# Gating unit of a two-layer decoder: layer norm on ScalarE, one block sum on VectorE, and another order of the same products

## The chip, the cores and the metric

The kernel runs on one core of one Trainium2 chip. The metric is the device time of one execution in microseconds (us). Three executions of the kernel before gave 807.21, 809.53 and 811.4 us; the median is 809.53 us. A profile was taken of one further execution. The engines have short names in the profile: PE is TensorE, DVE is VectorE, ACT is ScalarE, POOL is GpSimd, SP is SyncE, which here only issues transfers.

## What is computed

Two decoder layers over 512 tokens of width 1024, batch 1, float32. Each layer norms the tokens, scales and shifts them by columns that come from a conditioning vector (`ada_w`), mixes them, and then runs a squared-ReLU MLP of width 4096. Layer 0 mixes by windowed means. Layer 1 mixes by a gating unit, and this is the part that the change is about:

```python
def sgu_mixer(h, w_in, ln_g, ln_b, w_s, b_s, w_out):
    z = gelu(h @ w_in)                      # 512 x 2048
    u, v = split(z, 2)                      # 512 x 1024 each
    v = layernorm(v, ln_g, ln_b)            # over the 1024 features of a token
    v = v.reshape(B, 4, 128, 8, 128)        # 4 chunks of 128 tokens, 8 heads of 128 features
    mixed = einsum('hts,bnshc->bnthc', tril(w_s), v) + b_s
    gated = u * mixed
    return gated @ w_out
```

## The kernel before, in words

**Precision.** A float32 product is made of three fast ones. A weight tile is split into a high part `wh` (ACT copies it to the fast type) and a low part `wl` (DVE subtracts: `wl = raw - wh`); `split` does this for one 128x1024 tile. `split_d` does it without DVE: ACT writes `wh`, ACT writes `wl = -wh` into the low part's place, and POOL issues a transfer that adds the raw weights to it (an accumulating transfer). The list `LO` names the tiles that go the second way: the units u5 and u7 of the u half, and tiles o2 and o3 of the eight tiles of the output weights.

**The v half.** `v` is made by seven block products instead of eight (a Strassen-like scheme): the units v1, v2, v5, v6, v3, v7, v4, 24 matmuls of 128x512 each. Each takes a sum of blocks of the input (`hs`, made by `h_sum` from `hq`) and a sum of blocks of `w_v`. The weight sums build up in place in the tile `VB[0, 0]`: W00 for v1, then W01 is added for v5, then W11 for v6, then W10 for v4. Before the change each addition is an accumulating transfer of 1 MB from DRAM, which POOL issues once the two splits of the last sum have been read. v3 uses W11 alone (`VB[1, 1]`), v7 uses W01 + W11 in a third tile (`VB[0, 1]`). All these tiles are called `vb` in the profile.

**The u half and what follows.** u0 to u7 are products of 24 matmuls of 128x512 (u0 and u1 in two halves `a` and `b`). After a v block has its parts, ACT takes the Gelu in place; when a token tile of 128 tokens has both halves, `v_norm` norms it. Before the change DVE does this: `bn_stats` on both halves, `bn_aggr`, a small scalar step, POOL takes the power -0.5, and DVE applies mean and scale to 128x1024. `do_mix` (steps m0 to m7) multiplies the normed tokens by the triangular matrices, 4 matmuls each into one PSUM bank; `do_gate` (g0 to g7) multiplies with u and splits the result into the pair `gt`. Then come the products with `w_o`, in two halves of 4 weight tiles (`blocks(w_o[dh], dh)`: o0 to o3, o4 to o7), each over 4 token tiles of 24 matmuls.

**Columns.** While this runs, 24 columns of `ada_w` for the MLP are reduced: SP loads a 512 KB tile called `ada`, and one DVE instruction of 128x1024 makes the dot products. Most tiles lie in the pool `w4` with three buffers, which the raw `w_o` tiles (`raw`) use too.

**What sets the order.** PE runs strictly in the order of the code, that is of the string `SEQ`. Every other engine's order is made by `Plan.run`, a list scheduler that runs when the kernel is built: it takes the recorded instructions and its own costs and due times, and hands each engine the ready instruction with the earliest due time, and so settles the in-order queues of DVE, ACT, POOL and SP. One of its rules holds DVE free around a small POOL `tensor_tensor` (the power).

Of the kernel before, what the change touches and what calls it, by code (L numbers as in the profile page):

```python
# [7 lines left out]
F32 = mybir.dt.float32  # L8
F32R = mybir.dt.float32r
AF = mybir.ActivationFunctionType  # L10
# [4 lines left out]
P = 128  # L15
D = 1024
S = 512
# [57 lines left out]
class Plan:  # L75
# [129 lines left out]
    def run(self, lead):  # L205
# [63 lines left out]
            return True  # L269

        lock = {i for i, o in enumerate(ops) if o[0] == "POOL" and o[1] == "tensor_tensor"}
        gap = {i for i in lock if any(ops[j][0] == "DVE" for j in succs[i])}
        spot = {i: k for k, i in enumerate(pe)}
        sums = [0.0]
        for i in pe:
# [54 lines left out]
        while count < N:  # L330
            moved = True
            while moved:
                moved = False
                for e in ready:
                    if e == "DVE" and any(i in gap and when[i] <= now + 1e-9 and k - cost[i][1] < now + lead["gap"] for k, i in ready["POOL"]):
                        continue
                    if free[e] > now + 1e-9 or e == "SP" and sum(x[0] for x in lines[e]) > self.QUEUED or len(lines[e]) > 6:
                        continue
                    if e == "PE":
                        pick = pe[ppos] if ppos < len(pe) and not left[pe[ppos]] and when[pe[ppos]] <= now + 1e-9 and fits(pe[ppos]) else None  # L340
                    else:
                        pick, back = None, []
                        while ready[e]:
                            k, i = heapq.heappop(ready[e])
                            if when[i] <= now + 1e-9 and fits(i) and not (e in ("DVE", "ACT") and yields(e, i)) and not (i in lock and free["DVE"] > now + 1e-9):
                                pick = i
                                break
                            back.append((k, i))
                        for x in back:
                            heapq.heappush(ready[e], x)  # L350
                    if pick is None:
                        continue
                    i = pick
                    if e == "PE":
                        ppos += 1
                    for x in self.tiles[i]:
                        if x in place and x not in opened:
                            t, _ = place[x]
                            opened.add(x)
                            nxt[t] += 1  # L360
                            held[t] += 1
                    start[i] = now
                    if ops[i][1] == "dma_start":
                        issue = 0.85 if e == "POOL" else 0.35
                        free[e] = now + issue
                        flow(now)
                        row = min(x.free_size() for x in (*ops[i][3], *ops[i][4]))
                        lines[e].append([cost[i][0] + 0.01, cost[i][0] * min(1, 2048 / row), i])
                        landing()
                        end = now + cost[i][1] + sum(x[0] for x in lines[e][:-1])  # L370
                    else:
                        free[e] = now + cost[i][0]
                        end = now + cost[i][1]
                        if i in gap:
                            free["DVE"] = now + cost[i][0]
                        heapq.heappush(events, (end, i))
                    heapq.heappush(events, (free[e], -1))
                    soon[e].discard(i)
                    for j in succs[i]:
                        if i in self.preds[j]:  # L380
                            unstarted[j] -= i not in spot
# [12 lines left out]
            if i < 0:  # L394
                continue
            done[i] = now
            count += 1
            for x in self.tiles[i]:
                togo[x] -= 1
                if not togo[x] and tag[x] in held and (x in opened or x in before[tag[x]]):  # L400
                    held[tag[x]] -= 1
            for j in succs[i]:
                if i in self.preds[j]:
                    left[j] -= 1
                    hop = now + (0.0 if ops[i][0] == ops[j][0] else self.HOP)
# [13 lines left out]
def decoder_kernel(ctx: ExitStack, tc: tile.TileContext, xtok, vecs, fgrow, ada0, ada1, pool_w, w1s, w1, w1f, w1b, w2, w_v, w_u, w_o, wsT, ws, bs, out):  # L419
# [105 lines left out]
            V.tensor_tensor(l[:, c], r[:, c], f32(h[:, c]), ALU.subtract)  # L525
        return h, l

    LO = "u5 u7 o2 o3".split()

    def split_d(r, src=None):  # L530

# [1056 lines left out]
    def v_prep(m):  # L1588

        if m == 1:  # L1590
            VB[0, 0, 0] = vb0[0]
            VB[0, 0] = two(vb0[0])
        elif m == 2:
            v_load(1, 0)
        if m in (5, 6, 3, 7):
            h_sum(m)
        b = VB[{2: (1, 0), 3: (1, 1), 7: (0, 1)}.get(m, (0, 0))]
        src = {2: (1, 0), 3: (1, 1), 1: (0, 0)}.get(m)
        w = [split_d(b[q], src and wv_at(*src, q)) if f"v{m}{q}" in LO else split(b[q]) for q in range(2)]
        if m in (1, 5, 6):  # L1600
            G.dma_start(whole_(VB[0, 0, 0]), wv_at(*CHAIN_[{1: 5, 5: 6, 6: 4}[m]]), accum_op=ALU.add)
        if m == 5:
            v_load(1, 1)
        elif m == 3:
            v_load(0, 1)
            G.dma_start(whole_(VB[0, 1, 0]), wv_at(1, 1), accum_op=ALU.add)
        return w
# [3 lines left out]
    def v_run(m, w):  # L1611
# [14 lines left out]
        for hf in range(2):  # L1626
            po = banks[hf]
            r, n = {1: (0, 0), 5: (1, 1), 6: (0, 1), 3: (0, 1), 7: (1, 1), 2: (0, 0), 4: (1, 0)}[m]
            o = vt[2 * r + hf][:, n]
            if m in (1, 5) or m in (6, 3) and "v" not in half_:  # L1630
                A.activation(o, po, AF.Copy, scale=-1.0 if m == 6 else 1.0)
                if m in (6, 3) and hf:
                    half_.append("v")
                continue
            if m in (2, 3):
                V.tensor_tensor(o, o, po, ALU.add)
            elif m in (7, 6):
                V.tensor_tensor(o, o, po, ALU.subtract)
            A.activation(o, po if m == 4 else o, AF.Gelu)

    def v_norm(t):
        v = vt[t]
        stt = sm.tile([P, 2, V.BN_STATS_DIM], F32, name="stt", tag="stt")
        for ch in range(2):
            V.bn_stats(stt[:, ch, :], v[:, ch])
        ag = sm.tile([P, V.BN_AGGR_DIM], F32, name="ag", tag="ag")
        V.bn_aggr(ag, stt)
        r = rsqrt(ag[:, 1:2], 1.0, LN_EPS, 1)
        V.tensor_scalar(v, v, ag[:, 0:1], r, ALU.subtract, ALU.mult)

    ur = hx.tile([P, 2, D], F32, name="ur", tag="hx")
    wu, pu = {}, {}
# [74 lines left out]
    h_sums()  # L1727
    ready = {}
    cols = [modulation(q, get4 if q % 2 else get_gb) for q in range(24, 32)]
    cols += [modulation(q, get4) for q in range(32, 48)]  # L1730
    SEQ = "v1 v2 u0a u1a r0 u0b v5 u1b c2 u2 v6 c2 v3 c2 r1 v7 c2 u3 c1 n0 n1 v4 c1 n2 n3 c1 u4 c1 u5 m0 u6 m1 m2 c1 m3 g0 g1 u7 m4 g2 s0 g3 m5 m6 m7 g4 g5 g6 g7".split()
    prods = [x for x in SEQ if x[0] in "vu" and not x.endswith("b")]
    rs = []
    for x in SEQ:
# [32 lines left out]
    ex = cols  # L1767
    h_[0] = hparts()
    h32.append(featurewise("h32"))
    for dh in range(2):  # L1770
        wo = blocks(w_o[dh], dh)

        early = tuple(range(KD))
        n_ = 6 if dh == 0 else KD
# [1 line left out]
        for t, ks in [(t, early[:n_]) for t in range(3)] + [(t, early[n_:]) for t in range(3)] + [(3, early)]:  # L1776
# [4 lines left out]
            if early[-1] in ks:  # L1781
                gated(t, S * dh, S, pos[t])
                for _ in range(2):
                    if ex:
                        ex.pop(0)()
                if dh == 1 and t == 2:
                    normed(0, 1, 1)
                    spill(0)
# [137 lines left out]
```

## Time and profile before

| | |
|---|---|
| median of three executions | 809.53 us (807.21 to 811.4) |
| the profiled execution | 810.57 us, of which the span of the profile is 808.8 us |
| PE busy | 785.4 us (97% of the span) |
| DVE, ACT, POOL busy | 695.1, 520.6, 106.0 us |
| mean granted PE clock | 0.995 |
| gating unit, first v product to the last product with `w_o` | 361.34 to 500.24 us of the span |

A row of the timeline gives the start and length of an instruction in us, its engine, the source line (128 is the replay of all recorded instructions), what it writes and reads, and in brackets how long the engine stood idle before it and what ended that. PE ends are modelled: a 128x512 matmul is shown with 0.38 us although the next starts 0.22 us after it.

### The profile page before, as it was taken

Reading aid. Unit: us, or ns where it says so; the run is one execution under the profiler, and the core shown is the slowest. Engines: PE = TensorE matmul, PEld = TensorE weight load, DVE = VectorE, ACT = ScalarE, POOL = GpSimd, SP = SyncE. Lnnn points to the kernel's source line nnn. Section 1 sums busy time; section 2 is a strip of 40 time slices with the busy share of each in tenths; the row PEclk is TensorE's granted clock in tenths of the full one; section 3 lists DMA queues with packets and bytes.
Section 4 is the critical chain, followed back from the end, with each engine's and each line's share of the span. In section 5 each row is a group of like instructions: output and inputs, shape, how many; then the busy total and the mean of one; then the engine's idle time right before and its main releaser. Section 6 shows DMA issues by size and latency. Waiting matters only on the chain.

```text
span 808.8 us, 12689 instructions
## 1 busy us (share of the span) xinstructions
PE 785.4 (97%) x4893; PEld 710.4 (88%) x4893; DVE 695.1 (86%) x905; ACT 520.6 (64%) x739; POOL 106.0 (13%) x121
## 2 busy tenths in 40 slices
PE   6999999999999999999999999999999999999996
PEld 5778889999888888888788879999999988888885
DVE  5989699998789997997889888888778669888997
ACT  5486587776766666777554436778767676666672
POOL 4000000000001131250111101010000001112101
PEclk9999999999999999999999999999999999999998
DMA  9988959997999999345898976467876699899802
GB/s 344 417 307 307 345 205 274 279 289 190 313 317 211 245 233 269 144 151 163 202 254 278 300 237 209 160 187 234 253 217 179 173 279 269 191 227 206 218 1 104
DMA packets 48796, 189.67 MB, mean 234 GB/s; under 512 B 5440, under 2 KB 5600, under 8 KB 44896
## 3 DMA queue, kind: packets, MB, share of 16 engines
q1 hardware_dynamic: 36432, 128.81, 43.0%
q0 software_dynamic: 11872, 57.69, 35.0%
q10 hardware_dynamic: 432, 2.36, 0.7%
q8 instruction: 38, 0.62, 0.3%
q14 instruction: 22, 0.18, 0.1%
HBM read 182.53 MB, written 6.31 MB: 233 GB/s over the span
## 4 chain that ended last, share of the span: by engine, by line
PE 69%; DMA 11%; DVE 9%; issue 5%; ACT 4%; SPq 1%; POOLq 0%; POOL 0%; ACTq 0%; DVEq 0%
PE po L128 35%; PE pm L128 29%; DMA vb<-in_w_v 3%; DVE wl L128 3%; DMA ada<-in_ada 2%; ACT wh L128 2%; DMA bt<-in_w 2%; PE po L100 2%; PE px L100 1%; DMA raw<-in_w 1%; DMA x<-in_xtok 1%; ACT g L128 1%; DMA raw<-in_w_o 1%; PE pq L100 1%; DVE ada L100 1%
## 5 line engine op out<-in xcount | busy, mean ns | idle before, releaser
L128 PE MATMUL pm<-wh,op 128*128 128x512 f32 x896 | 267.9, 379 | 0.8 <-DVE op L128 0.6
L128 PE MATMUL po<-hb,wh 128*128 128x256 f32 (+1 forms) x1136 | 212.8, 291 | 0.2 <-DVE hb L128 0.2
L128 PEld LDWEIGHTS pm<-wh,op 128*128 128x128 f32 x896 | 169.3, 189 | 25.3 <-DVE op L128 1.0
L128 PEld LDWEIGHTS po<-hb,wh 128*128 128x128 f32 x1136 | 177.8, 192 | 5.1 <-DVE hb L128 0.4
L128 PE MATMUL pm<-wl,op 128*128 128x512 f32 x448 | 169.9, 379 | 0.8 <-DVE wl L128 0.8
L128 PE MATMUL po<-hb,wl 128*128 128x256 f32 (+1 forms) x569 | 163.4, 292 | 0.0
L128 PEld LDWEIGHTS po<-hb,wl 128*128 128x128 f32 x569 | 107.7, 192 | 2.9 <-DVE wl L128 0.4
L128 PE MATMUL po<-as,wh 128*128 128x256 f32 x576 | 97.1, 275 | 0.0
L128 PEld LDWEIGHTS pm<-wl,op 128*128 128x128 f32 x448 | 84.7, 189 | 13.0 <-DVE wl L128 1.1
L128 ACT ACTIVATE op<-g 128x1024 fp32r<-128x1024 f32 x56 | 59.0, 1056 | 54.3 <-PE pm L128 44.8
L128 DVE TENSOR_TENSOR wl<-bt,wh 128x1024 fp32r<-128x1024 f32 x64 | 78.2, 1236 | 14.4 <-ACT wh L128 14.3
L128 DVE TENSOR_TENSOR op<-g,op 128x1024 fp32r<-128x1024 f32 x56 | 68.5, 1225 | 22.0 <-ACT op L128 21.9
L128 PEld LDWEIGHTS po<-as,wh 128*128 128x128 f32 x576 | 87.4, 192 | 0.0
L128 ACT ACTIVATE wh<-bt 128x1024 fp32r<-128x1024 f32 x64 | 67.1, 1051 | 24.4 <-PE pm L128 12.4
L128 PE MATMUL po<-as,wl 128*128 128x256 f32 x288 | 79.3, 275 | 0.3 <-ACT g L128 0.3
L128 ACT ACTIVATE g<-g 128x512 f32<-128x512 f32 x100 | 61.1, 627 | 19.4 <-DVE g L128 18.3
L128 DVE SCALAR_TENSOR_TENSOR ada<-ada,cb 128x1024 f32<-128x1024 f32 x56 | 68.1, 1222 | 5.2 <-DMA ada<-in_ada 5.2
L128 DVE TENSOR_TENSOR wl<-tr,wh 128x1024 fp32r<-128x1024 f32 x48 | 58.6, 1223 | 10.5 <-ACT wh L128 10.3
L128 ACT ACTIVATE wh<-tr 128x1024 fp32r<-128x1024 f32 x48 | 50.8, 1058 | 25.5 <-PE po L128 14.1
L128 DVE TENSOR_TENSOR wl<-raw,wh 128x1024 fp32r<-128x1024 f32 (+1 forms) x44 | 50.2, 1150 | 11.9 <-ACT wh L128 11.9
L128 ACT ACTIVATE wh<-raw 128x1024 fp32r<-128x1024 f32 (+1 forms) x46 | 45.4, 998 | 22.1 <-DMA raw<-in_w_o 10.2
L128 PEld LDWEIGHTS po<-as,wl 128*128 128x128 f32 x288 | 55.3, 192 | 0.4 <-ACT g L128 0.4
(217 smaller groups left out, 1198.7 us busy)
## 6 DMA issues: line engine op xcount, KB each, us to landing
ada<-in_ada SPq DMA_DIRECT2D x76, 512.0 KB, 5.6
bt<-in_w POOLq DMA_DIRECT2D x22, 1024.0 KB, 9.5
yr<-in_w1b SPq DMA_DIRECT2D x22, 512.0 KB, 6.0
bt<-in_w SPq DMA_DIRECT2D x16, 512.0 KB, 8.3
b<-in_w SPq DMA_DIRECT2D x16, 512.0 KB, 8.2
raw<-in_w SPq DMA_DIRECT2D x13, 512.0 KB, 6.5
tr<-in_w1b SPq DMA_DIRECT2D x12, 512.0 KB, 6.3
raw<-in_w1b SPq DMA_DIRECT2D x12, 512.0 KB, 5.9
```

Of the source, the lines that this page charges most:

```text
L100: return f(*a, **kw)
L128: self.ops.append((name, attr, lambda: f(*a, **kw), out, ins, kw))
```

## The change

- `v_norm` goes from DVE to ACT. Every Gelu of v also sums its output (`accum_out`); DVE makes minus the mean of a token from two sums (tiny), ACT squares both halves with that as bias and sums the squares, DVE adds two sums, POOL takes the power, DVE makes the shift, and one ACT instruction of 128x1024 applies both.
- For v6 the weight sum is made by two DVE additions of `VB[1, 1]` to `VB[0, 0]` (128x1024 each), not by an accumulating transfer. Accumulating transfers are left for v5, v4 and v7.
- `LO` becomes o0, o1, u5, u7, v41 (v41 is the second weight tile of v4; its addend is read from `VB[0, 0]`, on chip).
- The second half of `w_o` is loaded inside the first half's products, and from the 13th column on the columns (`get_q`) use pairs in the pool `gq`, not `w4`.
- `SEQ` changes: u1b moves from before v6 to behind v3, u3 before v7, the norms and mixes move, u7 moves behind m5.
- In the planner, after a POOL power DVE first takes the instruction that waits for it.

```diff
-        gap = {i for i in lock if any(ops[j][0] == "DVE" for j in succs[i])}
+        gap = {i for i in sorted(lock)[:-NT] if any(ops[j][0] == "DVE" and i in self.preds[j] for j in succs[i])}
+        due = set()
...
+                            if e == "DVE" and due and i not in due:
+                                back.append((k, i))
+                                continue
...
                         if i in gap:
-                            free["DVE"] = now + cost[i][0]
+                            due.update(j for j in succs[i] if ops[j][0] == "DVE" and i in self.preds[j] and left[j] == 1 and fits(j))
+                        due.discard(i)
...
-    LO = "u5 u7 o2 o3".split()
+    LO = "o0 o1 u5 u7 v41".split()
...
-        if m in (1, 5, 6):
+        if m == 5 and True:
+            for q in range(2):
+                V.tensor_tensor(b[q], b[q], VB[1, 1][q], ALU.add)
+        elif m in (1, 5, 6):
             G.dma_start(whole_(VB[0, 0, 0]), wv_at(*CHAIN_[{1: 5, 5: 6, 6: 4}[m]]), accum_op=ALU.add)
-        if m == 5:
+        if m == 2:
             v_load(1, 1)
...
-            A.activation(o, po if m == 4 else o, AF.Gelu)
+            A.activation(o, po if m == 4 else o, AF.Gelu, accum_out=v_sum(2 * r + hf, n))
...
     def v_norm(t):
-        v = vt[t]
-        stt = sm.tile([P, 2, V.BN_STATS_DIM], F32, name="stt", tag="stt")
-        for ch in range(2):
-            V.bn_stats(stt[:, ch, :], v[:, ch])
-        ag = sm.tile([P, V.BN_AGGR_DIM], F32, name="ag", tag="ag")
-        V.bn_aggr(ag, stt)
-        r = rsqrt(ag[:, 1:2], 1.0, LN_EPS, 1)
-        V.tensor_scalar(v, v, ag[:, 0:1], r, ALU.subtract, ALU.mult)
+        v, s = vt[t], vs_[t]
+        c = [s[:, q : q + 1] for q in range(8)]
+        V.tensor_scalar(c[2], c[0], c[1], -(D**-1.5), ALU.add, ALU.mult)
+        for ch in range(2):
+            q = sm.tile([P, S], F32, name="tmp", tag="tmp")
+            A.activation(q, v[:, ch], AF.Square, bias=c[2], scale=D**-0.5, accum_out=c[3 + ch])
+        V.tensor_scalar(c[5], c[3], c[4], LN_EPS, ALU.add, ALU.add)
+        r = power(c[5], 1)
+        V.tensor_scalar(c[6], c[2], r, D**0.5, ALU.mult, ALU.mult)
+        A.activation(v, v, AF.Identity, bias=c[6], scale=r)
...
-    cols += [modulation(q, get4) for q in range(32, 48)]
-    SEQ = "v1 v2 u0a u1a r0 u0b v5 u1b c2 u2 v6 c2 v3 c2 r1 v7 c2 u3 c1 n0 n1 v4 c1 n2 n3 c1 u4 c1 u5 m0 u6 m1 m2 c1 m3 g0 g1 u7 m4 g2 s0 g3 m5 m6 m7 g4 g5 g6 g7".split()
+    cols += [modulation(q, get4 if q < 36 else get_q) for q in range(32, 48)]
+    SEQ = "v1 v2 u0a c1 u1a r0 u0b v5 c1 u2 v6 c1 c1 v3 u1b c1 r1 u3 v7 c1 c1 n0 v4 c1 c1 n2 n3 c1 n1 u4 c1 u5 u6 c1 m1 m0 m2 c1 m3 g0 g1 m4 s0 g2 g3 m5 u7 g4 m7 m6 g5 g6 g7".split()
...
+    wo_ = {0: blocks(w_o[0], 0)}
     for dh in range(2):
-        wo = blocks(w_o[dh], dh)
+        wo = wo_[dh]
...
+                if (dh, t) == (0, 2):
+                    wo_[1] = blocks(w_o[1], 1)
```

What this does to the queues is seen at three places. The first is DVE while PE runs u0b and v5. `hb` is the last piece of the normed input, which u0b reads; `hs` is the block sum for v5; `wl<-vb` is the low part of v5's weights. Before:

```order
L128 TENSOR_TENSOR hq_1311<-hq_1310,hq_1311 128x4x256
L128 TENSOR_TENSOR hb_1304<-hq_1310,hb_1302 128x2x256
L128 TENSOR_TENSOR wl_1348<-vb_1306,wh_1347 128x1024
L128 TENSOR_TENSOR hs_1346<-hq_1311,hs_1346 128x1024
L128 TENSOR_TENSOR wl_1350<-vb_1306,wh_1349 128x1024
L128 TENSOR_TENSOR wl_1357<-ur_1318,wh_1356 128x1024
L128 TENSOR_TENSOR ada_1345<-hq_1310 128x1024
```

The same place on DVE in the changed kernel (`vb_1306<-vb_1306,vb_1330` is the first of the two new additions):

```order
L128 TENSOR_TENSOR hq_1311<-hq_1310,hq_1311 128x4x256
L128 TENSOR_TENSOR wl_1353<-vb_1306,wh_1352 128x1024
L128 TENSOR_TENSOR hb_1304<-hq_1310,hb_1302 128x2x256
L128 TENSOR_TENSOR hs_1351<-hq_1311,hs_1351 128x1024
L128 TENSOR_TENSOR wl_1355<-vb_1306,wh_1354 128x1024
L128 TENSOR_TENSOR wl_1361<-ur_1318,wh_1360 128x1024
L128 SCALAR_TENSOR_TENSOR ada_1348,pmv_1349<-ada_1348,cb_103 128x1024
L128 TENSOR_TENSOR vb_1306<-vb_1306,vb_1330 128x1024
```

The piece `hb` has moved behind the split `wl<-vb`, and a column and the addition stand where the next block sum was.

The second place is ACT from the Gelus of v2 and v3 to the weights of v7 (`vb_1374` before, `vb_1376` after) and v4 (`vb_1306`). Before:

```order
L128 ACTIVATE u_1355<-po_1368 128x512
L128 ACTIVATE v_1317<-v_1317 128x512
L128 ACTIVATE v_1317<-po_1330 128x512
L128 ACTIVATE wh_1379<-vb_1374 128x1024
L128 ACTIVATE v_1317<-po_1331 128x512
L128 ACTIVATE wh_1381<-vb_1374 128x1024
L128 ACTIVATE wh_1390<-ur_1318 128x1024
L128 ACTIVATE line_1387<-pb_1386 8x128
L128 ACTIVATE v_1317<-v_1317 128x512
L128 ACTIVATE wh_1395<-vb_1306 128x1024
L128 ACTIVATE wh_1397<-vb_1306 128x1024
```

The same place on ACT in the changed kernel (`tmp,vs<-v,vs` are the squares of the norm of the first token tile, `u_1359<-po_1356` is the Gelu of u1):

```order
L128 ACTIVATE v_1317,vs_1343<-v_1317 128x512
L128 ACTIVATE v_1317,vs_1344<-v_1317 128x512
L128 ACTIVATE tmp_1403,vs_1343<-v_1317,vs_1343 128x512
L128 ACTIVATE tmp_1404,vs_1343<-v_1317,vs_1343 128x512
L128 ACTIVATE line_1385<-pb_1384 8x128
L128 ACTIVATE u_1359<-po_1356 128x512
L128 ACTIVATE wh_1389<-vb_1376 128x1024
L128 ACTIVATE wh_1391<-vb_1376 128x1024
L128 ACTIVATE wh_1394<-vb_1306 128x1024
L128 ACTIVATE wh_1396<-vb_1306 128x1024
L128 ACTIVATE wl_1397<-vb_1306 128x1024
```

Gelus, squares and four weight copies now stand ahead of `wl_1397`, the new second copy for v41. POOL's rows at this place, before:

```order
L128 DMA vb_1374<-in_w_v 128x2x1024
L128 DMA vb_1306<-in_w_v 128x2x1024
L128 DMA rowsum_1388<-line_1387 8x128
L128 DMA ada_1389<-rowsum_1388 128x1024
L128 DMA wl_1424<-in_w_u 128x1024
```

and on POOL in the changed kernel:

```order
L128 DMA vb_1306<-in_w_v 128x2x1024
L128 DMA vb_1376<-in_w_v 128x2x1024
L128 DMA rowsum_1386<-line_1385 8x128
L128 TENSOR_TENSOR rr_1405<-vs_1343,mhalf_82 128x1
L128 DMA ada_1387<-rowsum_1386 128x1024
L128 DMA wl_1397<-vb_1306 128x1024
L128 DMA wl_1422<-in_w_u 128x1024
```

The transfer for v6, which stood ahead of the first of these rows, is gone, v4's addition is issued ahead of v7's, and the addition for v41 stands behind the row sums.

The third place is SP, from the first tile of `w_o` on. Before:

```order
L128 DMA raw_1467<-in_w_o 128x1024
L128 DMA ada_1475<-in_ada1 128x1024
L128 DMA ada_1476<-in_ada1 128x1024
L128 DMA ada_1480<-in_ada1 128x1024
L128 DMA rg_1526<-in_w1b 128x1024 x2
L128 DMA ada_1481<-in_ada1 128x1024
L128 DMA ada_1485<-in_ada1 128x1024
L128 DMA ada_1486<-in_ada1 128x1024
L128 DMA ada_1491<-in_ada1 128x1024
L128 DMA ada_1492<-in_ada1 128x1024
L128 DMA raw_1494<-in_w_o 128x1024
```

and on SP in the changed kernel:

```order
L128 DMA raw_1467<-in_w_o 128x1024
L128 DMA raw_1485<-in_w_o 128x1024
L128 DMA ada_1475<-in_ada1 128x1024 x2
L128 DMA raw_1488<-in_w_o 128x1024
L128 DMA ada_1479<-in_ada1 128x1024 x2
L128 DMA raw_1491<-in_w_o 128x1024
L128 DMA ada_1483<-in_ada1 128x1024
L128 DMA raw_1494<-in_w_o 128x1024
```

The first row is o3 in both. The four tiles of the second half (before: the last row shown and the three behind it) stood behind eight columns; now o4 stands directly behind o3, and o5, o6 and o7 follow with one or two columns between them.

More of the change, by code (lines that the diff above doesn't have):

```diff
@@ L344, in run @@
                             k, i = heapq.heappop(ready[e])
-                            if when[i] <= now + 1e-9 and fits(i) and not (e in ("DVE", "ACT") and yields(e, i)) and not (i in lock and free["DVE"] > now + 1e-9):
+                            if e == "DVE" and due and i not in due:
+                                back.append((k, i))
+                                continue
+                            if when[i] <= now + 1e-9 and fits(i) and not (e in ("DVE", "ACT") and not due and yields(e, i)) and not (i in lock and free["DVE"] > now + 1e-9):
                                 pick = i
@@ L1638, in v_run, with v_sum @@
                 V.tensor_tensor(o, o, po, ALU.subtract)
-            A.activation(o, po if m == 4 else o, AF.Gelu)
+            A.activation(o, po if m == 4 else o, AF.Gelu, accum_out=v_sum(2 * r + hf, n))
+    vs_ = {}
+    def v_sum(t, n):
+        if t not in vs_:
+            vs_[t] = sm.tile([P, 8], F32, name="vs", tag=f"vs{t}", bufs=1)
+        return vs_[t][:, n : n + 1]
     def v_norm(t):
-        v = vt[t]
-        stt = sm.tile([P, 2, V.BN_STATS_DIM], F32, name="stt", tag="stt")
+        v, s = vt[t], vs_[t]
+        c = [s[:, q : q + 1] for q in range(8)]
+        V.tensor_scalar(c[2], c[0], c[1], -(D**-1.5), ALU.add, ALU.mult)
         for ch in range(2):
-            V.bn_stats(stt[:, ch, :], v[:, ch])
-        ag = sm.tile([P, V.BN_AGGR_DIM], F32, name="ag", tag="ag")
-        V.bn_aggr(ag, stt)
-        r = rsqrt(ag[:, 1:2], 1.0, LN_EPS, 1)
-        V.tensor_scalar(v, v, ag[:, 0:1], r, ALU.subtract, ALU.mult)
+            q = sm.tile([P, S], F32, name="tmp", tag="tmp")
[4 more added lines that the diff above has]
+        A.activation(v, v, AF.Identity, bias=c[6], scale=r)
     ur = hx.tile([P, 2, D], F32, name="ur", tag="hx")
@@ L1729, in decoder_kernel, with get_q @@
     cols = [modulation(q, get4 if q % 2 else get_gb) for q in range(24, 32)]
-    cols += [modulation(q, get4) for q in range(32, 48)]
-    SEQ = "v1 v2 u0a u1a r0 u0b v5 u1b c2 u2 v6 c2 v3 c2 r1 v7 c2 u3 c1 n0 n1 v4 c1 n2 n3 c1 u4 c1 u5 m0 u6 m1 m2 c1 m3 g0 g1 u7 m4 g2 s0 g3 m5 m6 m7 g4 g5 g6 g7".split()
+    pair_ = []
+    def get_q():
+        if not pair_:
+            t = gq.tile([P, 2, D], F32, name="ada", tag="g")
+            pair_.extend(t[:, q] for q in range(2))
+        return pair_.pop(0)
+    cols += [modulation(q, get4 if q < 36 else get_q) for q in range(32, 48)]
+    SEQ = "v1 v2 u0a c1 u1a r0 u0b v5 c1 u2 v6 c1 c1 v3 u1b c1 r1 u3 v7 c1 c1 n0 v4 c1 c1 n2 n3 c1 n1 u4 c1 u5 u6 c1 m1 m0 m2 c1 m3 g0 g1 m4 s0 g2 g3 m5 u7 g4 m7 m6 g5 g6 g7".split()
     prods = [x for x in SEQ if x[0] in "vu" and not x.endswith("b")]
```

## The prediction

> **What bounds the kernel now.** I read the page's engine totals first, then the chain of work that ended last, then a window over the stage that the change touches, and last PE's own rows there.
>
> ```profile
> span 808.8 us, 12689 instructions
> PE 785.4 (97%) x4893; PEld 710.4 (88%) x4893; DVE 695.1 (86%) x905; ACT 520.6 (64%) x739; POOL 106.0 (13%) x121
> PE 69%; DMA 11%; DVE 9%; issue 5%; ACT 4%; SPq 1%; POOLq 0%; POOL 0%; ACTq 0%; DVEq 0%
> core 0: us, PE busy (x) PEld busy (x) DVE busy (x) ACT busy (x) POOL busy (x), PEclk, DMA share, GB/s
> 361.34:500.24 138.90, 134.37 (x699) 117.33 (x698) 118.28 (x201) 72.08 (x107) 19.36 (x22) 0.99 0.80 239
> ```
>
> PE is busy for 97% of the span, and no PE product is added or removed by the change. So the change can gain only what PE stands idle or runs slowly, in the gating unit above all: up to there the two kernels have the same order. In this stage DVE is busy for 118.28 of 138.90 us and ACT for 72.08, so the work goes from the fuller engine to the emptier. But busy shares pay nothing; the waits of PE do. These are the ones of the stage, with some rows of PE beside them:
>
> ```profile
> 379.98 0.49 PE L128 MATMUL po<-hb,wh 128*128 128x256 f32 x2 [0.23 <-DVE hb L128]
> 382.35 0.45 PE L128 MATMUL po<-wh,hs 128*128 128x512 f32 x1 [0.20 <-DVE hs L128]
> 382.64 0.38 PE L128 MATMUL po<-wl,hs 128*128 128x512 f32 x1
> 387.39 0.38 PE L128 MATMUL po<-wh,hs 128*128 128x512 f32 x1
> 395.03 0.59 PE L128 MATMUL po<-hb,wh 128*128 128x512 f32 x2
> 396.66 0.48 PE L128 MATMUL po<-wh,hs 128*128 128x512 f32 x1 [1.03 <-ACT wh L128]
> 397.92 0.51 PE L128 MATMUL po<-wl,hs 128*128 128x512 f32 x1 [0.78 <-DVE wl L128]
> 462.03 0.45 PE L128 MATMUL po<-wh,gt 128*128 128x512 f32 x1 [0.56 <-DVE mods L128]
> 476.73 0.48 PE L128 MATMUL po<-wh,gt 128*128 128x512 f32 x1 [0.18 <-ACT wh L128]
> 477.99 0.48 PE L128 MATMUL po<-wl,gt 128*128 128x512 f32 x1 [0.78 <-DVE wl L128]
> 481.77 0.48 PE L128 MATMUL po<-wl,gt 128*128 128x512 f32 x1 [0.78 <-DVE wl L128]
> ```
>
> From 382.64 to 387.39 there are 22 matmuls, so one takes 4.75 / 22 = 0.216 us, though a row shows 0.38. A wait therefore costs its idle time and the modelled tail, 0.38 − 0.22 = 0.16. For v6: the pair at 395.03 would be followed at 395.46, and v6 starts at 396.66, 1.20 late; its second matmul, due at 396.88, starts at 397.92, 1.04 late. A unit of 24 matmuls is 5.2 us. Behind these two waits stands a second loss:
>
> ```profile
> 398.00:400.00 2.00, 2.00 (x6) 1.61 (x7) 2.00 (x2) 2.00 (x4) 1.23 (x2) 0.56 0.24 27
> 400.00:402.00 2.00, 2.00 (x7) 1.61 (x6) 1.87 (x3) 0.52 (x2) 0.49 (x1) 0.59 0.99 184
> ```
>
> The granted clock is 0.56 and 0.59 in these two stretches, so 2 × 0.44 + 2 × 0.41 = 1.70 us are lost.
>
> **The change part by part.** *The addition for v6.*
>
> ```profile
> 395.55 3.90 ACT L128 ACTIVATE wh<-vb 128x1024 fp32r<-128x1024 f32 x4 [3.69 <-DMA vb<-in_w_v]
> 397.33 1.20 POOL L128 DMA_DIRECT2D vb<-in_w_v  x1 [12.23 <-DMA vb<-in_w_v]
> 399.30 1.19 POOL L128 DMA_DIRECT2D vb<-in_w_v  x1 [0.77 <-DVE wl L128]
> DMA to landing us min/median/max: 9.5/12.7/13.9
> L128 DVE TENSOR_TENSOR hq<-hq 128x1024 f32<-128x1024 f32 x3 | 3.7, 1228 | 0.0
> ```
>
> ACT's first copy for v6 waited 3.69 us for the accumulating transfer, and DVE's subtraction for the copy: this is both waits. The transfer leaves; two additions of 1.23 us (the row of `hq`, same shape, both operands in SBUF) come, on DVE, which has had `W11` since the earlier load. Even right behind v5's splits they end long before 395.55. −2.24 us. With the idle time goes the low clock: −1.70.
>
> *Output weights.*
>
> ```profile
> 468.65 6.85 SPq L128 DMA_DIRECT2D raw<-in_w_o  x4
> 475.62 1.06 ACT L128 ACTIVATE wh<-raw 128x1024 fp32r<-128x1024 f32 x1 [1.73 <-DMA raw<-in_w_o]
> ```
>
> SP issued o4 to o7 from 468.65, behind eight columns. The wait at 476.73 and the two for low parts come from there, since the copy at 475.62 waited for the landing. Now o4 is issued right behind o3, and the others follow with at most two columns ahead of each, and columns have buffers of their own. The wait at 462.03 is named after a tiny `mods`; what ended with it is DVE's read of a PSUM bank behind three columns of 1.2 us, which now come later. All four go: 0.56 + 0.18 + 0.78 + 0.78 + 4 × 0.16 = −2.94. What is late next here is the split of o5 to o7, whose `wh` buffers come free only as the first half ends; I put that at 0, and its bound is one of today's waits, 0.94.
>
> *Norm.*
>
> ```profile
> L128 DVE BATCH_NORM_STATS2 stt<-v 128x6 f32<-128x512 f32 x8 | 5.5, 690 | 0.8 <-ACT v L128 0.7
> L128 DVE BATCH_NORM_AGGREGATE ag<-stt 128x2 f32<-128x12 f32 x4 | 0.8, 206 | 0.0
> L128 DVE TENSOR_SCALAR v<-v,ag,rr 128x1024 f32<-128x1024 f32 x4 | 3.1, 802 | 0.0
> L128 ACT ACTIVATE tmp<-x 128x512 f32<-128x512 f32 x8 | 5.0, 627 | 12.4 <-DVE x L128 10.9 <-DVE scl L128 1.5
> L128 ACT ACTIVATION_READ_ACCUMULATOR tmp<-x 128x1 f32 x8 | 1.5, 190 | 0.0
> L128 ACT ACTIVATE xs<-x,rr 128x1024 f32<-128x1024 f32 x2 | 2.3, 1140 | 0.0
> ```
>
> DVE loses 5.5 + 0.8 + 3.1 = 9.4 us and keeps some tiny steps. ACT gains eight squares (priced as `tmp<-x`, a square with a sum, 5.0), sixteen reads of a sum (8 × 0.19 for squares and 8 for Gelus: 3.0), four applications (priced as `xs<-x`, 1.14 each: 4.6), 12.6 us in all. This lies beside PE, in ACT's idle 138.9 − 72.1 = 66.8 us. Cost 0 as far as PE goes; but ACT is in order, and these steps stand ahead of weight copies, which comes next. The planner's rule moves tiny DVE steps behind a power: 0, bounds ±0.16, one such step.
>
> *`hb` behind a split.*
>
> ```profile
> 379.24 0.69 DVE L128 TENSOR_TENSOR hb<-hq,hb 128x512 fp32r<-128x512 f32 x1
> 379.84 1.22 DVE L128 TENSOR_TENSOR wl<-vb,wh 128x1024 fp32r<-128x1024 f32 x1
> 380.98 1.23 DVE L128 TENSOR_TENSOR hs<-hq,hs 128x1024 fp32r<-128x1024 f32 x1
> ```
>
> PE already waited for this `hb` (the row at 379.98). Behind the split it comes 380.98 − 379.84 = 1.14 later. u0b's rest, 382.35 − 0.36 − 379.98 = 2.0 us (its wait and tail of 0.16 taken off), then ends at 379.98 + 1.14 + 2.0 = 383.12, and v5, which began at 382.35, begins there, since `hs` is in time as before. +0.8.
>
> *v41's accumulation.* Its low part is ready only by ACT's copies, a POOL issue and a landing.
>
> ```profile
> 406.89 1.06 ACT L128 ACTIVATE wh<-vb 128x1024 fp32r<-128x1024 f32 x1 [2.07 <-DMA vb<-in_w_v]
> DMA to landing us min/median/max: 6.4/8.2/9.7
> 387.60 0.27 PE L128 MATMUL po<-hb,wl 128*128 128x256 f32 x1
> 390.28 0.38 PE L128 MATMUL po<-hb,wl 128*128 128x512 f32 x1
> ```
>
> Let S be v6's start and X = S + 10.4 the end of v3 (two units). Need: u1b takes 390.28 − 387.60 = 2.7 (the two rows are its first and what came behind it), u3 and v7 5.2 each, half of v4 2.6, so X + 15.7, with the small product ahead of u3 and the one high matmul X + 16.0. Supply: v6's second split ends near S + 1.2, POOL then issues v4's addition and 1.2 later v7's, near S + 2.6. At the median landing, 12.7 us (the 9.5/12.7/13.9 are the four `vb` transfers before), v7's weights are there at S + 15.3 = X + 4.9; ACT, with two Gelus, two squares, a row of sums and u1's Gelu behind v3 (about 4.2 us from X at the durations above), is there first. Four copies and the new negative copy at 0.96 each (the row of 3.90 for four) end at X + 9.7; 8.2 us to landing (four transfers of the same size, the `wl` of u5, u7, o2, o3) gives X + 17.9. So PE waits 1.9 us in the middle of v4. Bounds: with 9.5 for v7's sum ACT's own work decides, X + 9.0, and with 6.4 the landing is at X + 15.4: no wait. With 13.9 and 9.7 it is X + 20.6: 4.6. No row shows an accumulation whose source is on the chip; the nearest are the four quoted, from DRAM, and I take their median, 1.9. For u5 and u7 nothing changes; o0 and o1 in place of o2 and o3 are needed half a unit earlier, 0 to +1.5, taken as 0, because they are issued behind u6's Gelu, ahead of the last three units and all mixes.
>
> The sum: −2.24 − 1.70 − 2.94 + 0.8 + 1.9 = −4.2 us. The profiled execution took 810.57 (808.84 the span), 1.04 above the median of 809.53; against the median it gives 805.3.
>
> **Where a rule and the trace differ.** In this trace 2.24 us of idle time, in two pieces around one matmul, were followed by the half clock. The Trainium skill, "TensorE: Matmul & The Clock Gate", section "What's actually happening", lets the clock fall only after a whole idle window of about 3.4 us; by that neither the idle time here nor a wait of 1.9 in v4 would lower it, and the sum stays −4.2. By the trace, a slightly longer wait in v4 costs 1.70 more, −2.5. The trace decides that it can happen; that is the third case below.
>
> **The rivals.** *v41 is in time.* For it: 6.4 was seen, DMA has less to do with v6's 1 MB gone. Against it: the supply is 1.9 late at medians. It gives −6.1, so 803.4.
>
> *The lost clock comes back in v4.* If v41 lands after 9.7 instead of 8.2, or v7's sum at 13.9, the wait is about 3 us, longer than the idle time that was followed by the half clock at v6: −6.9 + 0.8 + 2.9 + 1.7 = −1.5, so 808.0. For it: v4's and v7's additions are issued together, as at 397.33 and 399.30, and the second of these was slow. Against it: one unbroken wait is another pattern.
>
> *Slower: the on-chip accumulation is far slower than one from DRAM.* Its place is the middle of v4, its price the landing less 8.2, beside the wait of 1.9 and the half clock: −6.9 + 0.8 + 1.9 + 1.7 + (L − 8.2). It passes +4 us from L = 14.8 on. At twice the median, 16.4, it gives +5.7 and 815.2. For it: nothing in the trace prices it. Against it: no 512 KB row is over 9.7, and even the 1 MB rows end at 13.9.
>
> **How the numbers follow.** A half per cent, 4.05 us, is about what a measurement of this kernel tells from no change. The forecast has 0.50, with a range of its own of 803.5 to 807 (each term by half a wait); v41 in time 0.15; the half clock again 0.25; the slow accumulation 0.10. 805.3 lies on the bound for faster (805.48), so of the forecast 0.31 is faster and 0.19 is the same. Faster: 0.31 + 0.15 = 0.46. The same: 0.19 + 0.24 = 0.43, and slower takes the rest, 0.11. The range of 802.5 to 810.5 goes from the second case with a microsecond of spread to the third with 2.5, leaving out the slow accumulation and a little at the lower end.
>
> **What the changed profile would show.** No PE wait at v6's start, and a clock of 1.00 through v6 and v3; `vb<-vb` on DVE twice. A wait of some 1.4 us `<-DVE hb` in u0b. One wait of about 1.9 in the middle of v4, ended by a transfer or by `wl`, and the clock behind it. No wait in the second half of `w_o`, and ACT's copies of o4 to o7 waiting for buffers, not for transfers. Groups of squares and applications on ACT, no `BATCH_NORM` in the stage. I would be wrong if units beyond these wait: v7 for its own weights, m1 for the norm on ACT, or o0's low part behind the Gelus.

## The result and the profile after

The changed kernel takes 801.56 us in the median of six runs (800.96 to 803.25), the kernel before 809.84 in six runs beside it, and 808.6 to 809.0 in the larger sets of runs that came with the experiments. The ratio is 0.9908, with a 95% interval of 0.9885 to 0.9931: 7 to 8 us faster. The forecast was 805.3, in a range of 802.5 to 810.5. So the sign was right, and the gain came out 3 to 4 us larger than forecast, with a time just outside of the range.

The page of the changed kernel, first the span and the engines, then the chain that ended last, then the window over the same stage, from v1 to the last product with `w_o`, and the waits of PE in it:

```profile
span 799.3 us, 12696 instructions
PE 781.3 (98%) x4893; PEld 708.4 (89%) x4893; DVE 690.7 (86%) x898; ACT 531.7 (67%) x768; POOL 106.3 (13%) x121
PE 83%; DMA 6%; DVE 5%; issue 3%; ACT 3%; SPq 0%; POOL 0%; POOLq 0%; DVEq 0%; ACTq 0%
...
359.31:491.83 132.52, 131.44 (x700) 116.08 (x698) 114.13 (x194) 83.39 (x138) 18.84 (x22) 1.00 0.77 247
...
PE po L128 <- DMA wl<-in_w_o: 0.5, 1, 0.5
PE px L128 <- ACT xs L128: 0.4, 1, 0.4
PE po L128 <- DVE v L128: 0.2, 1, 0.2
```

The stage is 132.52 us long instead of 138.90, with a granted clock of 1.00 instead of 0.99. PE waits 1.1 us in it, in three small places. None of the eight waits of before is left, and none of those that the forecast put in their place has come. DVE's share of the chain fell from 9% to 5%, that of the transfers from 11% to 6%.

The two spans differ by 9.5 us, of which the stage is 6.4. Ahead of it 2.0 us are gone, where the work is the same: before, v1 starts at 361.34, after at 359.31. That is scatter of the one profiled execution of before: a second profile of the same kernel has v1 at 359.76, and in the twelve profiles of other experiments it starts at 358.0 to 360.6. The last 1.1 us lie behind the stage: 308.6 us from its end to the end of the span before, 307.5 after, and 308.8 to 309.0 in the second profile of before and in the four variants of the changed kernel that gain as much, so I take this too for scatter of one profile.

### The profile page after: what moved, and what is told of

Same layout as the page of the kernel before. It is cut to its first block, busy times and chain, and to the rows that moved or that the text cites. A ratio compares the mean times of both kernels' runs of the same rounds, so it can differ in the third digit from the quotient of the medians.

```text
span 799.3 us, 12696 instructions
## 1 busy us (share of the span) xinstructions
PE 781.3 (98%) x4893; PEld 708.4 (89%) x4893; DVE 690.7 (86%) x898; ACT 531.7 (67%) x768; POOL 106.3 (13%) x121
## 4 chain that ended last, share of the span: by engine, by line
PE 83%; DMA 6%; DVE 5%; issue 3%; ACT 3%; SPq 0%; POOL 0%; POOLq 0%; DVEq 0%; ACTq 0%
PE po L128 41%; PE pm L128 36%; PE po L100 2%; DMA ada<-in_ada 1%; DMA raw<-in_w 1%; PE px L100 1%; DMA wl<-in_w_o 1%; DMA x<-in_xtok 1%; PE pq L100 1%; DVE ada L100 1%; ACT wh L128 1%; DVE wl L128 1%; DMA yr<-in_w1b 1%; PE px L128 1%; ACT tmp L128 1%
## 5 line engine op out<-in xcount | busy, mean ns | idle before, releaser
L128 DVE TENSOR_TENSOR wl<-raw,wh 128x1024 fp32r<-128x1024 f32 (+1 forms) x44 | 51.9, 1184 | 8.2 <-ACT wh L128 8.1
```

Of the source, the lines that this page charges most:

```text
L128: self.ops.append((name, attr, lambda: f(*a, **kw), out, ins, kw))
```

## Experiments

The kernel before has medians of 808.6 to 809.0 us beside these runs. Ratios are to it; differences in us are to the changed kernel's 801.56, except where said.

**One part alone: v6's additions.**

```diff
-        if m in (1, 5, 6):
+        if m == 5 and True:
+            for q in range(2):
+                V.tensor_tensor(b[q], b[q], VB[1, 1][q], ALU.add)
+        elif m in (1, 5, 6):
...
-        if m == 5:
+        if m == 2:
             v_load(1, 1)
```

> The kernel before with one part of the change alone: v6's weight sum made by two DVE additions, and W11 loaded one unit earlier. Theory (the gain is the PE waits that each part takes away, part by part): no wait at v6, no half clock behind it, the waits in w_o stay: 2.24 + 1.70 = 3.9 us under the kernel before. Rival (DVE is too full without the move of the norm to ACT, so that the additions make other splits late): the waits at v6 stay in part or come up at v3 or v7, less than 2 us gained.

It takes 813.51 us, 1.0065 (1.0045 to 1.0084) times the kernel before: slower. The waits at v6 are gone, and another came at v7. From the timelines of PE, ACT, DVE and POOL, back from the wait, with the landing times of POOL's two transfers:

```profile
410.31 0.79 PE L128 MATMUL po<-wh,hs 128*128 128x512 f32 x1 [5.59 <-ACT wh L128]
409.22 1.99 ACT L128 ACTIVATE wh<-vb 128x1024 fp32r<-128x1024 f32 x2
408.09 1.23 ACT L128 ACTIVATE v<-v 128x512 f32<-128x512 f32 x2 [3.06 <-DVE v L128]
406.22 1.23 DVE L128 SCALAR_TENSOR_TENSOR ada<-ada,cb 128x1024 f32<-128x1024 f32 x1 [5.17 <-DMA ada<-in_ada]
391.35 2.45 POOL L128 DMA_DIRECT2D vb<-in_w_v  x2 [26.90 <-DVE wl L128]
DMA to landing us min/median/max: 8.5/11.9/15.2
```

Two things stand behind the 5.59 us. v7's sum is issued right behind v4's now, at 392.1, and the slower of the two landings, 15.2 us, would have it there at 407.3, where v7 could begin at 404.7. Before, it had a start of 2 us on v4's and landed in 9.5. And the copies start not at 407.3 but at 409.2: ACT holds them behind two Gelus, these wait for DVE's additions to `v`, and DVE is held by a column whose tile lands at 406.2 and which is not needed before the MLP. The half clock follows: 0.50 in the windows from 410 to 416. The rival had a wait at v7, but for a full DVE; neither expectation named these two causes.

**One part alone: the early load of w_o**, with `wo_[1] = blocks(w_o[1], 1)` in the first half's third token tile and `get_q` for columns from the 13th on.

> The kernel before with one part alone: the second half of w_o loaded inside the first half's products, and the columns from the 13th on in the pool gq. Theory (part by part): the three waits in the second half of w_o go (1.74 + 3 x 0.16 = 2.2 us), and the one at 462.03 (0.72) goes as well if the columns no longer stand ahead of the gates on DVE; -2.2 to -2.9 us. Rival (the early load needs the emptier DVE or the other order): under 1 us gained.

It takes 825.3 us, 1.0202 (1.0181 to 1.0224). PE's largest wait, and POOL's rows ahead of it:

```profile
464.77 0.76 PE L128 MATMUL po<-wl,gt 128*128 128x512 f32 x1 [8.92 <-DMA wl<-in_w_o]
453.29 0.56 POOL L128 DMA_DIRECT2D gb<-gainm  x1 [3.11 <-DMA gainm<-line]
453.88 1.81 POOL L128 DMA_DIRECT2D wl<-in_w_o  x2
```

The accumulations of o2 and o3 are issued only at 453.9, behind a small broadcast that waited for another transfer; ACT, too, writes their negative copies only from 452.30 on, behind a gate that waited for DVE. Some 6 us more of this run lie behind the stage: PE waits 4.08 us at 709.69, in the MLP (`<-DVE op`), and the clock is 0.56 and 0.66 in the 4.3 us that follow. Why that wait came stays open; the following run does not have it, and moves both accumulations:

**The early load with another list.**

```diff
-    LO = "u5 u7 o2 o3".split()
+    LO = "o0 o1 u5 u7".split()
```

> The kernel before with the early w_o load, the pool gq and LO with o0, o1 in place of o2, o3. Theory (the 16.7 us that the early load alone cost were the accumulations of o2 and o3, issued by POOL only behind the gain row's broadcast at 453, 8.9 us of idle time and a half clock): 10 us or more of them gone, and within 4 us of the kernel before. Rival (the columns that now load elsewhere, or the other raw loads, make it): still 8 us or more over the kernel before.

805.04 us, 0.9959 (0.9946 to 0.9972): 20.3 us less than the run above, and 3.6 under the kernel before. POOL issues the two now at 441.4 and 444.0, each right behind ACT's copy and ahead of the broadcast. From the start of the `w_o` products to the layer's last transposes this run needs 3.0 us less than the profile of before (51.53 against 54.53), which is the size of the forecast's term of 2.94. So the early load pays only with o0 and o1 in the list.

**The changed kernel with v6's transfer again.**

```diff
-        if m == 5 and True:
-            for q in range(2):
-                V.tensor_tensor(b[q], b[q], VB[1, 1][q], ALU.add)
-        elif m in (1, 5, 6):
+        if m in (1, 5, 6):
```

> The changed kernel with v6's weight sum by an accumulating transfer again, all else as changed. Theory (part by part): the two waits at v6 come back, and the half clock with them, so 2.2 to 3.9 us over the changed kernel. Rival (the other order, with u1b behind v3, or the transfer landing sooner, hides it): within 1 us. v6 starts 2.7 us earlier behind v5 here than in the kernel before, because u1b no longer stands ahead of it, so the wait may even be longer, up to 2.7 us more.

807.11 us, 5.6 more than the changed kernel. Its waits at v6, and the window that follows:

```profile
392.52 0.58 PE L128 MATMUL po<-wh,hs 128*128 128x512 f32 x1 [2.19 <-ACT wh L128]
393.78 0.79 PE L128 MATMUL po<-wl,hs 128*128 128x512 f32 x1 [0.68 <-DVE wl L128]
...
392.52:400.00 7.48, 6.80 (x17) 5.17 (x18) 5.78 (x6) 5.27 (x6) 2.38 (x2) 0.54 0.60 103
```

Counted from v1, v6 starts 2.3 us later than in the changed kernel, its second matmul 1.0 later still, and up to v4 another 2.8 us go to a clock of 0.54. Both of v6's terms are there, and larger than in the kernel before, since u1b no longer covers the transfer.

**The changed kernel with the old SEQ.** The edit is the one line.

> The changed kernel with the string SEQ of the kernel before, all else as changed. Theory A (the order only moves work about): within 1.5 us. Theory B (with v7 right behind v3, its weights are late, as in the run that had v6's additions alone: 5.6 us of idle time before v7): slower by 4 us or more, with a wait for wh or wl at v7's start.

809.85 us, 8.3 more than the changed kernel. PE waits 5.34 us at v7, as with the additions alone. DVE's row shows the same column, and the landings the same pair:

```profile
410.48 0.79 PE L128 MATMUL po<-wh,hs 128*128 128x512 f32 x1 [5.34 <-ACT wh L128]
406.23 1.23 DVE L128 SCALAR_TENSOR_TENSOR ada<-ada,cb 128x1024 f32<-128x1024 f32 x1 [6.20 <-DMA ada<-in_ada]
DMA to landing us min/median/max: 8.2/11.5/14.8
```

Theory B holds. In the changed kernel the second transfer of the pair takes 14.4 us as well, and a column waits for its tile on DVE as well (3.12 us of idle time at 405.43); but u1b and u3, 7.9 us of products, stand between v3 and v7, and DVE's additions to `v` are done before that column. v7 waits for nothing there.

**The changed kernel with the late load of w_o.** The undone edit of the second experiment, with LO as changed.

> The changed kernel with the second half of w_o loaded between the halves again and the columns in the pool w4. Theory (part by part): the waits in the second half of w_o come back, 2.2 to 2.9 us slower. Rival (the early load is worth more or less than the waits of the profile before): outside of that.

805.14 us, 3.6 more than the changed kernel. The waits of the second half do not come back; in their place there is one wait, in the first half, and a low clock behind it:

```profile
462.83 0.48 PE L128 MATMUL po<-wh,gt 128*128 128x512 f32 x1 [1.95 <-DVE gt L128]
460.94 1.22 DVE L128 SCALAR_TENSOR_TENSOR ada<-ada,cb 128x1024 f32<-128x1024 f32 x1
463.00:465.00 2.00, 2.00 (x8) 1.62 (x9) 1.59 (x3) 0.00 (x0) 0.00 (x0) 0.73 0.97 354
465.00:467.00 2.00, 2.00 (x6) 1.60 (x5) 1.37 (x3) 0.01 (x1) 0.00 (x0) 0.50 0.91 356
```

DVE takes three columns among the last gates (the last of them is the second row; the first waits 1.49 us for its tile), and PE stands until a gate is split. So the rival holds: undoing this part costs more than the term, and by another way. What I had named as the cause, the late landing of o4 to o7, ends no wait of PE here; columns ahead of gates on DVE do.

**The changed kernel with v41's low part by DVE.**

```diff
-    LO = "o0 o1 u5 u7 v41".split()
+    LO = "o0 o1 u5 u7".split()
```

> The changed kernel with v41's low part by DVE again (LO is o0 o1 u5 u7). Theory (v41's accumulation was in time within 0.1 us in the one profile, and costs nothing in most executions): same time within 1 us, and one DVE instruction of 1.22 us more. Rival (v41 is late in some executions, as forecast): 1 to 2 us faster than the changed kernel in the median. Second rival (DVE needs that relief): slower by 1 us or more, with a wait for wl at v4 or u4.

801.22 us, as the changed kernel. What the forecast took for the change's largest cost, 1.9 us, is nothing here. In the changed kernel's own trace, ACT's copies, POOL's issue, its landing, and PE's first matmul that needs it:

```profile
405.07 3.90 ACT L128 ACTIVATE wh<-vb 128x1024 fp32r<-128x1024 f32 x4 [0.32 <-DMA vb<-in_w_v]
408.88 1.04 ACT L128 ACTIVATE wl<-vb 128x1024 fp32r<-128x1024 f32 x1
410.22 0.89 POOL L128 DMA_DIRECT2D wl<-vb  x1 [1.95 <-DVE wl L128]
DMA to landing us min/median/max: 7.2/7.2/7.2
417.46 0.48 PE L128 MATMUL po<-wl,hb 128*128 128x512 f32 x1
```

It lands at 410.22 + 7.2 = 417.4, and the matmul starts at 417.46, 0.1 late by the length of its row.

**The changed kernel with the norm on DVE.** `v_norm` as before, and the Gelus without sums.

> The changed kernel with the norm of v on DVE again (bn_stats, bn_aggr, one application per token tile), the Gelus without sums. Theory A (the move to ACT by itself is worth nothing to PE; the gain came from v6's sum, the order and the early w_o): within 1.5 us of the changed kernel. Theory B (the 9.4 us taken from DVE are what makes the order hold: DVE was busy for 5.75 to 8.7 of each 10 us in the middle of the changed stage): slower by 3 us or more, with waits of PE that end with wl or v by DVE.

810.83 us, 9.3 more than the changed kernel: PE's wait in v4, and POOL's rows and the one of DVE that lead to it:

```profile
423.08 0.79 PE L128 MATMUL po<-wl,hb 128*128 128x512 f32 x1 [5.29 <-DMA wl<-vb]
413.23 0.93 POOL L128 DMA_DIRECT2D wl<-vb  x1
412.67 0.58 POOL L128 DMA_DIRECT2D ada<-rowsum  x1 [4.46 <-DMA rowsum<-line]
407.22 0.99 POOL L128 DMA_DIRECT2D rowsum<-line  x1
406.69 0.56 POOL L128 TENSOR_TENSOR rr<-rv,mhalf 128x1 f32<-128x1 f32 x1 [15.13 <-DVE rv L128]
404.99 1.23 DVE L128 SCALAR_TENSOR_TENSOR ada<-ada,cb 128x1024 f32<-128x1024 f32 x1 [2.85 <-DMA ada<-in_ada]
```

It looks like a verdict for theory B, but it is the wait that the forecast had placed at v41, only longer. DVE's column, which waits for its tile, holds the norm's small steps ahead of the power; POOL's power waits for these, the row sums stand behind the power, and v41's transfer stands behind the broadcast of the row sums. Counted from v1, it is issued 3.4 us later than in the changed kernel, and it takes 9.8 us to land. Whether the norm itself costs anything, the next run tells.

**Norm on DVE, and v41 by DVE too.** Both edits above.

> The changed kernel with the norm on DVE and, beside that, v41's low part by DVE too. Theory A (the 9.3 us that the norm on DVE cost were the late accumulation for v41 and the half clock behind it: POOL's power stood ahead of the row sums, and these ahead of that accumulation): without v41's accumulation most of it is gone, within 3 us of the changed kernel. Theory B (DVE itself is too full with the norm, 9.4 us more and 1.2 for v41): 5 us or more slower than the changed kernel, with waits of PE for wl or v by DVE.

801.55 us. Theory A holds: the 9.4 us of DVE work that the norm takes, and the 12.6 that ACT pays for it, are worth nothing to PE, as the forecast said. v41's accumulation is what makes the norm's place matter, and it brings nothing itself.

**The changed kernel with the planner's old rule.** The two places of the planner in the diff are undone.

> The changed kernel with the planner's old rule around POOL's power (DVE held free for its length), nothing else undone. Theory: the rule moves only tiny steps and costs nothing, within 1 us. Rival (holding DVE for some 0.6 to 1 us at each of some 30 powers shifts enough to make a split late): 1 to 4 us slower.

801.41 us: no difference in the medians. The profiles show a small one, which the next section names.

**v6's additions with the new SEQ, and nothing else.**

> The kernel before with v6's additions by DVE and the new SEQ, nothing else. Theory (the additions bring v4's and v7's transfers into one moment, and v7 must then stand further behind v3, which is what the new SEQ does): no wait at v6 and none at v7; the w_o waits stay; 3 to 5 us under the kernel before, where the additions alone were 5 us over it. Rival (the norm on DVE makes other splits late in this order): no gain, with waits for wl or v by DVE in v7 or v4.

809.48 us, 1.0013 (1.0000 to 1.0026): no gain. Yet no wait of more than 0.23 us is left from v1 to u4. Up to the first product with `w_o` the run has gained: 89.03 us from v1 against 92.08 and 91.47 in the two profiles of before. It then loses it again:

```profile
454.48 0.45 PE L128 MATMUL po<-wl,gt 128*128 128x512 f32 x1 [3.57 <-DMA wl<-in_w_o]
```

This is o2's accumulation, as in the run with the early load. PE comes earlier to a transfer that is issued no earlier: 86.4 us behind v1, against 85.5 before.

**The three parts together.** v6's additions, the new SEQ and the w_o part (early load, `get_q`, LO with o0, o1, u5, u7); norm, v41 and planner as before.

> The kernel before with v6's additions, the new SEQ and the w_o part (early load, columns in gq, LO with o0, o1, u5, u7); the norm stays on DVE, v41's low part too, and the planner is the old one. Theory (these parts are the whole gain; the forecast's 6.9 us of waits and half clock, with no cost beside them): within 1 us of the changed kernel, some 7 us under the kernel before. Rival (norm and planner carry a part that a neighbour hid in the single runs): 2 us or more slower than the changed kernel.

802.36 us (800.19 to 803.87), 0.9924 (0.9905 to 0.9944): the whole gain, within what can be told. In its profile only the wait of 0.2 us `<-DVE v` is left in the stage. No version of these runs is clearly faster than the changed kernel.

**The kernel before, profiled again** (one execution).

> The kernel before, profiled once more. Theory (about 2 us of the profiled execution of before, ahead of v1, were that execution's own: in nine other profiles, whose work up to there is the same, v1 starts at 358.2 to 360.6 us, and there at 361.34): v1 starts below 361, and the waits at v6, 1.0 and 0.8 us, and in the second half of w_o come again. Rival (the change itself moves v1's start): v1 starts at 361 or later.

810.12 us, span 808.4, v1 at 359.76. PE's waits at v6 are there again with 1.08 and 0.78 us. In `w_o` there are four, one of them new:

```profile
460.18 0.45 PE L128 MATMUL po<-wh,gt 128*128 128x512 f32 x1 [0.90 <-DVE mods L128]
474.16 0.48 PE L128 MATMUL po<-wl,gt 128*128 128x512 f32 x1 [0.57 <-DVE wl L128]
476.81 0.48 PE L128 MATMUL po<-wl,gt 128*128 128x512 f32 x1 [0.78 <-DVE wl L128]
480.67 0.48 PE L128 MATMUL po<-wl,gt 128*128 128x512 f32 x1 [0.78 <-DVE wl L128]
```

The two waits in u0b and at v5, 0.23 and 0.20, are not.

## Why the forecast was right, and where it was wrong

**v6's waits and the low clock (−2.24 − 1.70): right.** Between v5's start and v4's the same units stand in both kernels: 420.32 − 382.35 = 37.97 us before, 414.58 − 380.08 = 34.50 after. That is 3.47 less, with a new wait of 0.22 + 0.16 in it, so 3.85 of 3.94. Undone alone, the term is 5.6 us, because the new order took away u1b's cover; done alone it is a loss, because v7 needs the new order: with that order, v6's additions leave no wait above 0.16 us at v6 or v7.

**w_o (−2.94): right in size, half right in cause.** From the first product with `w_o` to the first transposes behind, 39.89 us became 37.06: −2.83. The late load gave back 3.6 us, by columns ahead of gates and a half clock, not by late tiles of `w_o`. The copies of o6 and o7 wait for PE to free a buffer (0.24 us each), not for a transfer, as forecast. The wait of 0.45 us at 450.04 is for the low part of o1: with its tail 0.6 us, in a term that I had taken as 0 with bounds of 0 to +1.5.

**Norm (0): right.** Shown by the run with the norm on DVE beside v41 undone.

**Planner (0, bounds ±0.16): too small, and below what the medians tell.** All seven profiles with the new rule have a wait of 0.40 or 0.41 us at the first transposes (`px`, 8.3 us behind v1's start), `<-ACT xs`, and none of the eight with the old rule has it. With its tail that is +0.57 us.

**hb behind a split (+0.8): the step that failed first.** From v1 to v5 it is 21.01 and 20.38 us in the two profiles of before, and 20.77 after. In the 20.77 is the planner's 0.57, which also gives `hb` that much more time. Three runs have the same split ahead of `hb` and the old rule (the planner's, v6's additions with the new SEQ, the three parts together): v5 starts at 20.15 in each, and PE does not wait for `hb`. So the term measures −0.9 against the profile that I used, and −0.2 against the second one. I added 1.14 us to a time of `hb` that I took as fixed by DVE's order. But that time was set by a transfer: ACT's copy of v5's weights stands ahead of ACT's `hq` piece, and waited for the sum to land.

```profile
374.98 1.06 ACT L128 ACTIVATE wh<-vb 128x1024 fp32r<-128x1024 f32 x1 [2.14 <-DMA vb<-in_w_v]
371.88 1.07 ACT L128 ACTIVATE wh<-vb 128x1024 fp32r<-128x1024 f32 x1 [0.32 <-DMA vb<-in_w_v]
377.29 0.69 DVE L128 TENSOR_TENSOR hb<-hq,hb 128x512 fp32r<-128x512 f32 x1
```

The first row is of before, the other two of after. From v1's start that copy runs at 13.64 us before and at 12.57 after, and `hb` starts at 17.90 before and at 17.98 after, though a split was put ahead of it. The second profile of before has 13.02 there and no wait of PE at `hb` at all. So the wait that I built on does not stand in every execution of before. The sum comes sooner with the new SEQ: in all nine profiles with it that copy starts 11.4 to 12.6 us behind v1 and waits for the sum 0.32 us at most, and in the six with the old SEQ it starts at 12.9 to 14.3 and waits 0.6 to 2.8 us. In the new order one of the two loads of `w_v` behind the sum is issued 2.0 or 4.4 us behind v1, not right behind it. No run moved this load alone, so it is not shown that this is the cause.

**v41 (+1.9): the term that was mis-sized.** The run without it shows that it costs nothing. Three pieces of the 1.9: v7's sum was there 0.8 us earlier than I put it (ACT's copies start 4.1 us behind v3, not 4.9), the accumulation landed in 7.2 us and not 8.2, and v4 itself began 0.4 us later, by a wait for DVE's addition to `v`; 0.3 us that POOL's issue starts behind the copy, and that I had left out, goes the other way. v7's sum was issued 2.4 us earlier than I put it (390.7 for v6's start + 2.6 = 393.1) and landed more slowly, in 14.4 and not 12.7:

```profile
389.63 2.44 POOL L128 DMA_DIRECT2D vb<-in_w_v  x2 [23.00 <-DVE wl L128]
DMA to landing us min/median/max: 8.3/11.3/14.4
```

Six kernels had this transfer, and it landed in 6.4, 6.5, 6.8, 7.1, 7.2 and 9.8 us. The nearest rows, with a source in DRAM, had given 6.4 to 9.7. I took their middle; an accumulation from a tile on the chip sat at their lower end in five of six. The second case, "v41 is in time", was the one that came, with a chance of 0.15.

**The sum.** Of the 3.7 us between forecast and result, 2.7 are these two costs, which did not come. The waits and the clock alone are −6.9. The stage says −6.4 against the first profile of before, with 1.1 us of small new waits in it, and 139.73 − 132.52 = −7.2 against the second. The runs' medians say −7.0 to −8.3. Taken against the median, −6.9 gives 802.6. The 1.1 us left to 801.56 are no more than one stretch of before differs between its two profiles (39.89 and 40.98 us from the first product with `w_o` to the transposes); no run says more about them.

**The half clock again in v4.** It did not come in the changed kernel. The run with the norm on DVE shows the case itself: 5.29 us of wait, and a clock of 0.57 in the 6.92 us that follow.

## What to carry to other kernels

Undone alone, the parts cost 5.6, 8.3, 9.3 and 3.6 us, together more than three times the whole gain; done alone, two of them made the kernel slower. In a kernel of strictly ordered queues the price of an edit is that of the next thing in the queue, so a part is judged with its neighbours in place and undone beside what it touches, and a large loss from undoing one part is read from the wait that came up, not put down to the part. Before an operation with no deadline (a column here) is placed ahead of one with a deadline, look at what it waits for itself: a late tile on DVE held ACT, POOL or PE in four of these kernels.

## What the runs showed of the hardware

The half clock came after waits of about 2 us. A single wait of 1.95 us (the late load of `w_o`) brought it: 0.73 and 0.50 in the two windows from 463, 2 × 0.27 + 2 × 0.50 = 1.5 us lost in these alone, so that this wait cost nearly twice its length. Two waits of 1.0 to 1.1 and 0.78 us around one matmul brought it in four profiles of four (both of before, and the two with the early load alone). Single waits up to 1.36 us did not: seven profiles have one of 1.05 to 1.36 us between 532 and 543, and the clock behind each is 1.00 (the 1.36 at 540.75, in the run with v6's transfer again). The Trainium skill, "TensorE: Matmul & The Clock Gate", section "What's actually happening", asks for a whole idle window of about 3.4 us; the runs differ, and here the runs decide.

Accumulating transfers that POOL issues close together come in far apart. In all fifteen profiles v4's and v7's, 1 MB each and issued 0.8 to 2 us apart, land one in 8.1 to 9.5 us and the other in 13.7 to 16.1.
